# Two pairs of small tables merged, and the weight buffers behind them moved by 64 bytes

## The chip, the core and the metric

The kernel runs on one core of one Trainium2 chip. The metric is the device time of one execution in microseconds. The time before is the median of three runs. One further execution was recorded by the hardware profiler, and all rows below are from that one.

## What is computed

Two transformer-like blocks run one after the other on 256 tokens with 1024 features, all in float32. The first has chunked attention, a gated linear recurrence, a merge of the two branches, and a feed-forward layer; the second has four feed-forward layers, a gating unit with a layer norm over 2048 features, and stick-breaking attention with shared keys and values. Cut to what matters here:

```python
def first_block(x, ...):
    xn = rmsnorm(h, norm_mix_g)
    q, k, v, xr, gr, ga, gb = jnp.split(xn @ w_in, splits, axis=-1)
    ya = chunked_band_attention(q, k, v, rel_table) @ w_attn_out
    hr = rg_lru(causal_depthwise_conv(xr, conv_w, conv_b), ...)
    yb = (hr * jax.nn.gelu(gr)) @ w_rnn_out
    h = h + (g_a * ya + g_b * yb) @ w_o
    g, up = jnp.split(rmsnorm(h, norm_ffn_g) @ w_ffn_in, 2, axis=-1)
    h = h + (jax.nn.silu(g) * up) @ w_ffn_out

def second_block(x, ...):
    # twice: swiglu, then (gating unit | stick-breaking attention), then swiglu
    x = x + 0.5 * swiglu(rms_norm(x, ffn_norm), ffn_w_in, ffn_w_out)
    x = x + chunked_sgu(h, a_w_in, a_ln_g, a_ln_b, a_w_s, a_b_s, a_w_out)
    x = x + stick_breaking_attention(q, k_shared, v_shared) @ b_w_o
```

Nearly all the arithmetic is products of the 256 tokens with large weight matrices.

## The kernel before

Every weight is read once, in 239 pieces of 1 MB (128 partitions x 2048 floats), in an order written out by hand (`PLAN`). `load` (L142 to L150) takes the next of three `raw` buffers and issues its DMA from SyncE. A piece has two chunks of 1024 columns. `prep` (L152 to L171) splits a chunk into two float32r tiles: `h`, a rounded copy that ScalarE makes (L165), and `l`, the difference `raw - h` that VectorE makes (L166). There are eight buffers of `h` and eight of `l`. Splitting runs up to seven chunks ahead of the matmuls.

An activation is split in the same way, into `xh` and `xl`, or into pairs of the four tiles `rr0` to `rr3`. A product is three matmuls that add up in PSUM (`mm3`, L215): high x high, high x low, low x high. All go through `mm` (L213). Rows of the profile name a matmul as out<-moving,stationary. There are two kinds. In `pe_k`, `pe_a` and `pe_r` the weights (`h`, `l`) are stationary, 128 columns of them, and 256 columns of an activation move (`acc<-rr,h`, `wk<-xh,h`). In `pe_nat` and `pe_rn` the activation is stationary and 512 columns of weights move (`wk<-h,xh`, `acc<-h,rr`). In the stage of keys and values (`kv_emit`) both kinds alternate with 256 columns each. Between them stand transposes (L755) and the matmuls of the attentions.

All tiles outside PSUM that live through the kernel come from one pool (`sb`, L133), one behind the other in the order in which the code asks for them: the parameters `par`, the residual `x0` to `x3`, `xh`, `xl`, `rr0` to `rr3`, the slab `sa`, the slabs `sb` to `sh`, two 128x128 tables, and then the small tables, among them `mhalf` (the exponent -0.5 for the power on GpSimd, L283), `tiny` (a bias of the square root at L688), `mv` and `rstd` (mean, variance and its power in the gating unit, L1070 to L1077), and the tables `ntri` and `nones` of the stick-breaking attention. Behind this pool lie the three buffers of `raw`, then the eight of `h`, then the eight of `l`. So the sizes of the small tables decide where the weights lie. An address is a number of bytes inside each partition.

Of the kernel before, what the change touches and what calls it, by code (L numbers as in the profile page):

```python
# [109 lines left out]
class Builder:  # L110
# [210 lines left out]
    def setup(self):  # L321
        nc, dram = self.nc, self.dram
        self.P = self.sb("par", [128, 224])[:, 0:NPAR]
        self.X = [self.sb(f"x{p}", [128, 2, 256]) for p in range(4)]
        self.XS = (self.sb("xh", [128, 8, 256], F32R), self.sb("xl", [128, 8, 256], F32R))
        self.RR = [self.sb(f"rr{i}", [128, 8, 256], F32R) for i in range(4)]
        self.SA = self.sb("sa", [128, 2080])[:, 0:8 * 259]
        self.SL = {c: self.sb("s" + c, [128, 2048]) for c in "bcdfgh"}
        self.ident = self.sb("ident", [128, 128])
        self.ones = self.sb("ones", [128, 128])  # L330
        self.mhalf = self.sb("mhalf", [128, 2])
        self.Rt = self.sb("rt", [128, 256])
        self.R1 = self.sb("r1t", [128, 256])
        self.Rkv = self.sb("rkv", [128, 256])
        self.rckv = self.sb("rckv", [128, 2])
        self.v2 = self.sb("v2", [128, 2])
        self.rc = self.sb("rc", [128, 2])
        self.tiny = self.sb("tiny", [128, 1])
        self.rc05 = self.sb("rc05", [128, 2])
        self.c8 = self.sb("c8", [128, 8])  # L340
        self.nc8 = self.sb("nc8", [128, 8])
        self.half = self.sb("half", [128, 24])
        self.sq = self.view("b", 4)
        nc.scalar.dma_start(self.P, dram["par"])
        x_load = lambda p: nc.sync.dma_start(self.X[p], dram["x"][:, 2 * p:2 * p + 2, :])
        for f in range(2):
            nc.sync.dma_start(self.X[0][:, f, :], dram["x"][:, f, :])
        self.warm_up()
        for g in range(2):
            t = self.rawp.tile([128, 2048], F32, tag="raw", name="raw")  # L350
            for c in range(2):
                if 2 * g + c:
                    x_load(2 * g + c)
                n = 512 if 2 * g + c == 0 else 1024
                for o in range(c * 1024, (c + 1) * 1024, n):
                    nc.sync.dma_start(t[:, o:o + n], dram["w"][g, :, o:o + n])
            self.raw[g] = t
        self.loads = 2
        self.load()
        self.gw = self.SL["h"].rearrange("p (a b) -> p a b", b=128)  # L360
        make_identity(nc, self.ident)
        nc.gpsimd.memset(self.ones, 1.0)
        nc.gpsimd.memset(self.mhalf, -0.5)
        nc.gpsimd.memset(self.tiny, 2.0 ** -115)

    def warm_up(self):
# [658 lines left out]
    def sgu(self, fin, fin_l):  # L1025
        nc, dram, P = self.nc, self.dram, self.par
# [6 lines left out]
        rs = SL["b"][:, 0:1024]  # L1033
        bs = SL["b"][:, 1024:2048]
        st6 = self.sb("bn6", [128, 2, 4, 6])
        mv = self.sb("mv", [128, 2, 2])
        rstd = self.sb("rstd", [128, 2])
        nc.gpsimd.dma_start(ws, dram["ws"])
        nc.gpsimd.affine_select(out=ws, in_=ws, pattern=[[0, 8], [1, 128]], compare_op=ALU.is_ge, fill=0.0,
                                base=0, channel_multiplier=-1)  # L1040
# [54 lines left out]
        a = ("A", "a_in")  # L1095
# [310 lines left out]
```

## Time and profile before

| | |
|---|---|
| time, median of 3 runs | 1444.81 us (1444.66 to 1446.23) |
| the profiled execution, its own time | 1445.04 us |
| its span, first to last instruction | 1443.3 us |
| TensorE busy with matmuls | 1431.0 us, 9112 instructions |
| VectorE busy | 875.1 us |
| ScalarE busy | 732.0 us |
| GpSimd busy | 21.4 us |
| read from HBM | 257.53 MB, 179 GB/s |

Matmuls are pipelined: one is listed from its start to its modelled end, and the next starts long before that. The length of one is therefore not what it costs; the distance from start to start is. Where the chain that ended last shows a run of matmuls without a break, the length of the run over their number is that distance.

### The profile page before, as it was taken

What the parts mean: (1) busy time and instruction counts of PE and PEld (TensorE: products, weight loads), DVE (VectorE), ACT (ScalarE), POOL (GpSimd) and SP (SyncE); (2) the same over time, 40 slices, a digit from 0 to 9 for tenths busy, and PEclk for the clock granted to TensorE, in tenths of its full rate; (3) what the DMA queues carried; (4) which work ended last, traced back from release to release, by engine and by line L of the source; (5) the groups of instructions that cost most, each with busy time, mean ns of one, the idle gap of its engine ahead of it and who ended that gap; (6) DMA issues with size and microseconds to landing.
All of it is one profiled execution on the core that took longest, in us unless ns stands there. A gap on an engine that the chain in (4) does not pass through costs nothing.

```text
span 1443.3 us, 21730 instructions
## 1 busy us (share of the span) xinstructions
PE 1431.0 (99%) x9112; PEld 1277.2 (88%) x9112; DVE 875.1 (61%) x1102; ACT 732.0 (51%) x985; POOL 21.4 (1%) x57
## 2 busy tenths in 40 slices
PE   8999999999999999999999999999999999999998
PEld 8998989888888888898999888898888898888886
DVE  6976688655547555566775554457555477644453
ACT  5777465544445544455444544446444467544442
POOL 0000000000000000000000000000000000000000
PEclk9999999999999999999999999999999999999999
DMA  7555545554553545546444555545554542445440
GB/s 296 197 193 200 186 160 195 188 201 175 184 195 147 204 176 180 209 151 224 171 168 155 222 185 180 191 154 204 186 193 176 183 168 88 161 176 193 186 175 30
DMA packets 37602, 259.98 MB, mean 180 GB/s; under 512 B 4224, under 2 KB 4608, under 8 KB 7040
## 3 DMA queue, kind: packets, MB, share of 16 engines
q1 hardware_dynamic: 36288, 253.77, 48.3%
q0 software_dynamic: 1072, 4.72, 1.0%
q8 instruction: 71, 1.16, 0.3%
q14 instruction: 27, 0.22, 0.0%
q10 hardware_dynamic: 144, 0.10, 0.0%
HBM read 257.53 MB, written 1.05 MB: 179 GB/s over the span
## 4 chain that ended last, share of the span: by engine, by line
PE 97%; DVE 1%; DMA 0%; ACT 0%; issue 0%; POOL 0%; SPq 0%; POOLq 0%; DVEq 0%; ACTq 0%
PE wk L213 60%; PE acc L213 35%; PE wk L755 2%; DMA raw<-w 0%; DVE l L166 0%; PE acc L525 0%; ACT h L165 0%; DVE sd L275 0%; DVE sb L275 0%; PE wk L525 0%; POOL r1c L283 0%; ACT sf L1020 0%; DVE sf L1011 0%; ACT sd L1010 0%; DVE sa L747 0%
## 5 line engine op out<-in xcount | busy, mean ns | idle before, releaser
L166 DVE TENSOR_TENSOR l<-raw,h 128x1024 fp32r<-128x1024 f32 (+1 forms) x479 | 572.7, 1220 | 317.2 <-ACT h L165 316.7
L165 ACT ACTIVATE h<-raw 128x1024 fp32r<-128x1024 f32 (+1 forms) x479 | 495.3, 1053 | 303.5 <-PE wk L213 192.7
L213 PE MATMUL wk<-h,xh 128*128 128x512 f32 x912 | 361.9, 397 | 0.0
L213 PE MATMUL wk<-h,xl 128*128 128x512 f32 x912 | 359.6, 394 | 0.0
L213 PE MATMUL wk<-l,xh 128*128 128x512 f32 x912 | 359.2, 394 | 0.0
L213 PE MATMUL acc<-rr,h 128*128 128x256 f32 x2016 | 358.5, 281 | 0.0
L213 PEld LDWEIGHTS acc<-rr,h 128*128 128x128 f32 x2016 | 307.9, 188 | 3.6 <-issue 1.9
L213 PE MATMUL acc<-rr,l 128*128 128x256 f32 x1008 | 281.2, 279 | 0.0
L213 PEld LDWEIGHTS wk<-h,xl 128*128 128x128 f32 x912 | 171.8, 188 | 39.4
L213 PEld LDWEIGHTS wk<-l,xh 128*128 128x128 f32 x912 | 171.9, 189 | 37.2
L213 PEld LDWEIGHTS wk<-h,xh 128*128 128x128 f32 x912 | 171.9, 188 | 36.8
L213 PEld LDWEIGHTS acc<-rr,l 128*128 128x128 f32 x1008 | 190.0, 189 | 0.0
L213 PE MATMUL wk<-xh,h 128*128 128x256 f32 x512 | 145.5, 284 | 2.0 <-ACT h L165 2.0
L213 PE MATMUL wk<-xh,l 128*128 128x256 f32 x512 | 143.2, 280 | 1.0 <-DVE l L166 1.0
L213 PE MATMUL wk<-xl,h 128*128 128x256 f32 x512 | 143.0, 279 | 0.0
L213 PEld LDWEIGHTS wk<-xh,h 128*128 128x128 f32 x512 | 96.1, 188 | 4.6 <-ACT h L165 2.4
L213 PEld LDWEIGHTS wk<-xh,l 128*128 128x128 f32 x512 | 97.2, 190 | 1.4 <-DVE l L166 1.4
L213 PEld LDWEIGHTS wk<-xl,h 128*128 128x128 f32 x512 | 96.5, 188 | 0.2
L312 ACT ACTIVATE rr<-wk 128x512 fp32r<-128x512 f32 (+1 forms) x63 | 35.9, 569 | 113.9 <-PE wk L755 109.2
L313 DVE TENSOR_TENSOR rr<-wk,rr 128x512 fp32r<-128x512 f32 (+1 forms) x63 | 41.4, 657 | 77.8 <-ACT rr L312 77.8
L743 ACT ACTIVATE sg<-wk,rc 128x512 f32<-128x512 f32 (+1 forms) x48 | 30.8, 652 | 75.6 <-PE wk L213 67.8
L747 DVE SCALAR_TENSOR_TENSOR sa<-wk,rc,sg 128x512 f32<-128x512 f32 (+1 forms) x48 | 32.3, 706 | 53.7 <-PE wk L213 50.0
(256 smaller groups left out, 1167.3 us busy)
## 6 DMA issues: line engine op xcount, KB each, us to landing
raw<-w SPq DMA_DIRECT2D x237, 1024.0 KB, 4.8
sd<-bias POOLq DMA_DIRECT2D x8, 384.0 KB, 3.3
raw<-w SPq DMA_DIRECT2D x3, 512.0 KB, 7.7
sh<-gates SPq DMA_DIRECT2D x1, 1024.0 KB, 9.0
out<-sf SPq DMA_DIRECT2D x4, 256.0 KB, 2.2
x<-x SPq DMA_DIRECT2D x3, 256.0 KB, 6.9
raw<-w SPq DMA_DIRECT2D x2, 256.0 KB, 4.3
sa<-ws POOLq DMA_DIRECT2D x1, 512.0 KB, 5.3
```

What stands on the lines that cost most here:

```text
L165: nc.scalar.activation(h[:, s], raw[:, s], AF.Copy)
L166: nc.vector.tensor_tensor(l[:, s], raw[:, s], h[:, s].bitcast(F32), op=ALU.subtract)
L213: self.nc.tensor.matmul(out, lhsT, rhs, start=start, stop=stop, skip_group_check=True)
L312: self.nc.scalar.activation(zh, src, AF.Copy)
L313: self.nc.vector.tensor_tensor(zl, src, zh.bitcast(F32), op=ALU.subtract)
L743: nc.scalar.activation(SG[i][t][:, 0:w], src, AF.Silu, scale=self.rcol[:, t:t + 1])
L747: nc.vector.scalar_tensor_tensor(Z[i][t][:, 0:w], src, s, SG[i][t][:, 0:w], op0=ALU.mult, op1=ALU.mult)
L755: nc.tensor.transpose(bank[:, f, t * 128:(t + 1) * 128], Z[i][t][:, o:o + 128], self.ident)
```

## The change

The tile `tiny` (one column) becomes the third column of `mhalf`. The tile `rstd` (two columns) becomes the last two of a tile of six columns whose first four are `mv`. The memset of `mhalf` is limited to its first two columns. Every tile that is asked for after these lies lower by what they took, and so do `raw`, `h` and `l`.

```diff
@@ setup @@
-        self.mhalf = self.sb("mhalf", [128, 2])
+        self.mhalf = self.sb("mhalf", [128, 3])
...
-        self.tiny = self.sb("tiny", [128, 1])
+        self.tiny = self.mhalf[:, 2:3]
...
-        nc.gpsimd.memset(self.mhalf, -0.5)
+        nc.gpsimd.memset(self.mhalf[:, 0:2], -0.5)
         nc.gpsimd.memset(self.tiny, 2.0 ** -115)
@@ sgu @@
-        mv = self.sb("mv", [128, 2, 2])
-        rstd = self.sb("rstd", [128, 2])
+        mr = self.sb("mv", [128, 6])
+        mv, rstd = mr[:, 0:4].rearrange("p (a b) -> p a b", b=2), mr[:, 4:6]
```

## Rows read from the trace of the kernel before

**Rows 1.** The page's busy time and chain, and the cores: span, granted clock.
```profile
PE 1431.0 (99%) x9112; PEld 1277.2 (88%) x9112; DVE 875.1 (61%) x1102; ACT 732.0 (51%) x985; POOL 21.4 (1%) x57
...
PE 97%; DVE 1%; DMA 0%; ACT 0%; issue 0%; POOL 0%; SPq 0%; POOLq 0%; DVEq 0%; ACTq 0%
...
core 0: 1443.3 us, clock 0.998
```
**Rows 2.** The chain in order of time: start us, length us, what, number.
```profile
159.75 8.16 PE wk L213 x72
...
334.84 22.40 PE wk L213 x96
...
747.20 36.75 PE acc L213 x312
...
1324.09 21.97 PE wk L213 x96
```
**Rows 3.** Timeline around 300 us: start us, length us, engine, instruction.
```profile
300.50 0.40 PE L213 MATMUL wk<-h,xl 128*128 128x512 f32 x1
300.50 0.19 PEld L213 LDWEIGHTS wk<-h,xh 128*128 128x128 f32 x1
```
**Rows 4.** Groups by line, shapes apart: number | busy us, mean ns | idle.
```profile
L213 PE MATMUL wk<-h,xh 128*128 128x512 f32 x912 | 361.9, 397 | 0.0
...
L213 PE MATMUL acc<-rr,h 128*128 128x256 f32 x2016 | 358.5, 281 | 0.0
...
L213 PE MATMUL acc<-rr,l 128*128 128x256 f32 x1008 | 281.2, 279 | 0.0
...
L213 PE MATMUL wk<-xh,h 128*128 128x256 f32 x512 | 145.5, 284 | 2.0 <-ACT h L165 2.0
...
L213 PE MATMUL acc<-h,rr 128*128 128x512 f32 x176 | 57.7, 397 | 0.0
...
L213 PE MATMUL acc<-l,rr 128*128 128x512 f32 x88 | 34.2, 389 | 0.0
```
**Rows 5.** Timeline of TensorE's matmuls in the stage of keys and values.
```profile
1162.00 0.28 PE L213 MATMUL acc<-rr,l 128*128 128x256 f32 x1
1162.12 0.28 PE L213 MATMUL acc<-h,rr 128*128 128x256 f32 x1
...
1162.83 0.40 PE L213 MATMUL acc<-rr,h 128*128 128x256 f32 x2
...
1163.41 0.28 PE L213 MATMUL acc<-rr,l 128*128 128x256 f32 x1
1163.52 0.28 PE L213 MATMUL acc<-h,rr 128*128 128x256 f32 x1
...
1163.98 0.28 PE L213 MATMUL acc<-l,rr 128*128 128x256 f32 x1
```
**Rows 6.** Single lines of ScalarE and VectorE: ns min/median/max, first and last start.
```profile
L165 ACT ACTIVATE h<-raw x479: 629/1058/1081, 5.9 to 1413.8; 128x1024 fp32r<-128x1024 f32 x159, 128x512 fp32r<-128x512 f32 x1
...
L166 DVE TENSOR_TENSOR l<-raw,h x479: 693/1224/1228, 6.6 to 1415.6; 128x1024 fp32r<-128x1024 f32 x159, 128x512 fp32r<-128x512 f32 x1
...
L682 ACT ACTIVATE sa<-sc x2: 1041/1042/1042, 86.2 to 88.2; 128x1024 f32<-128x1024 f32 x2
...
L684 DVE SCALAR_TENSOR_TENSOR sb<-sa,sb x2: 1217/1218/1220, 90.8 to 93.0; 128x1024 f32<-128x1024 f32 x2
```
**Rows 7.** The tile `rstd`: its writer and its first reader.
```profile
L1077 DVE TENSOR_SCALAR sc<-sc,mv,rstd x4: 539/541/544, 693.1 to 698.9; 128x512 f32<-128x512 f32 x4
...
L283 POOL TENSOR_TENSOR rstd<-v,mhalf x1: 719/719/719, 690.6 to 690.6; 128x2 f32<-128x2 f32 x1
```
**Rows 8.** The chain's first load, and the waits of ScalarE for loads.
```profile
3.14 6.71 DMA raw<-w
...
ACT h L165 <- DMA raw<-w: 9.8, 9, 2.7
```

## The prediction

> **What bounds the kernel now.** I read the page's busy table and its chain first [rows 1]. TensorE is busy for 1431.0 of the 1443.3 us, 97% of the chain that ended last lies on it, and its granted clock was 0.998, so the upper of its two levels, 2.4 GHz. Nothing that happens on another engine or in a queue moves the end unless TensorE waits for it, and TensorE waits almost nowhere. What is left to ask is the pace of the matmuls themselves, so the second view is the chain in order of time, where a piece is a run of matmuls without a break: its length over its count is the pace of one matmul [rows 2].
>
> The pace comes in pairs. With 256 columns it is 8.16 us / 72 = 113.3 ns in one piece and 36.75 / 312 = 117.8 ns in another. With 512 columns it is 21.97 / 96 = 228.9 ns and 22.40 / 96 = 233.3 ns. In the chain a long piece keeps one of the two from end to end and a new one may have the other; in the first four feed-forward stages there are twelve pieces of 96 at 22.40 us, in the last stage three of 96 at 21.97. Two things follow. The quicker and the slower pace differ by the same amount, 4.5 and 4.4 ns, at either length, so it is a charge per matmul and not per column. And 256 more columns cost 228.9 - 113.3 = 115.6 or 233.3 - 117.8 = 115.5 ns, 0.451 ns a column, where one column per cycle would be 1/2.4 = 0.417 ns. Something other than the count of cycles sets the pace, and the operands of these matmuls are just what the change moves.
>
> The third view shows what runs at once: the weight load of the next matmul starts in the same hundredth of a microsecond as the matmul before it [rows 3]. So TensorE reads two streams at a time, the moving operand of one matmul and the stationary operand of the next. In nearly all matmuls one of the two is a split weight (`h`, `l`) and the other an activation (`xh`, `xl`, `rr`).
>
> **The change part by part.** *Does it move them?* Each table takes its bytes per partition rounded up to 32. From `x0` to the first `raw` the sizes add up to 121,408 bytes = 237 x 512 + 64. `mhalf` grows from 8 to 12 bytes and stays in 32, `tiny` goes (-32); `mv` grows from 16 to 24 and stays in 32, `rstd` goes (-32). The sum is then 121,344 = 237 x 512. Buffers of `raw` are 8192 bytes apart, those of `h` and `l` 4096, so all 19 move with it. `x`, `xh`, `xl`, `rr`, `sa` and the `s` slabs lie ahead of the small tables and stay. `ntri` and `nones` move by 32 bytes; they serve 64 matmuls only.
>
> *Instructions.* None is added or removed. The two POOL memsets of `mhalf` and `tiny` stay two. The only new ties are that a reader of one half of a merged table may be held for the writer of the other half. For `mhalf`/`tiny` both writers are memsets at the start. For `mv`/`rstd` the power on POOL starts at 690.6 us for 719 ns and needs the variance made from `mv` anyway; its first reader on VectorE starts at 693.1 us [rows 7]. That leaves 693.1 - 691.3 = 1.8 us, so an added tie costs 0; without that cover it would be below 1 us, once.
>
> *The split on ScalarE and VectorE.* 479 copies `h<-raw` have a median of 1058 ns, 479 differences `l<-raw,h` one of 1224 ns, at 64 past. The nearest rows with other places in the 512 bytes are a 128x1024 copy-like activation from 128 past to 0 past, 1041 to 1042 ns, and a 128x1024 VectorE operation at 128 and 0 past, 1217 to 1220 ns [rows 6]. At most the change gives back 16 and 6 ns a piece, or takes as much: 479 x 0.016 = 7.7 us on ScalarE, which has 48% of the span free. On the path stands one such pair, ahead of the first matmul: 0.02 us. I take 0.
>
> *The loads.* 1 MB loads write rows of 8 KB at the new place. ScalarE waited for `raw` 9.8 us in total, 9 times, and on the chain a load stands once, 6.71 us at the start [rows 8]. A load dearer or cheaper by 1% would be 0.07 us there. I take 0.
>
> *The matmuls.* These carry the sum. With 256 columns there are 2016 + 1008 + 3 x 512 [rows 4], and in seven smaller groups of the same kind 192 + 96 + 3 x 64 + 32 + 16: 5088. With 512 there are 3 x 912 + 176 + 88 and three groups of 64: 3192. If each pace held half of them, they would take 5088 x 115.55 + 3192 x 231.1 = 587.9 + 737.7 = 1325.6 us of the span (an estimate: the pieces show both paces in like amounts). All at the quicker pace they would take 576.5 + 730.6 = 1307.1 us, 18.5 less; all at the slower 599.4 + 744.7 = 1344.1 us, 18.5 more. With one column per cycle, 106.7 and 213.3 ns, they would take 542.9 + 680.9 = 1223.8 us, 101.8 less. So the bounds of this term are -102 and +18.5 us, and all hangs on whether a place in the 512 bytes matters to the pace.
>
> For that the trace has three rows that bear on it. First, absolute place: in the 256-column runs the moving operand is at 0 and the stationary one at 64, in the 512-column runs the other way round, and both show the same two paces, 4.4 ns apart. In the `kv` stage the same 256 columns stand both ways side by side [rows 5]: with `h` and `l` moving, six matmuls in 1162.83 - 1162.12 = 0.71 us, 118 ns; on the next pass four in 1163.98 - 1163.52 = 0.46 us, 115 ns; and the six with `rr` moving between them take 0.69 us, 115 ns. So which of the two lies at 64 is all one. Second, relative place: only at a handover are both streams at 0, when `rr,l` runs while the weights of `h,rr` load. It took 0.12 us in the slower stretch and 0.11 us in the quicker [rows 5], what its neighbours took. One matmul with both at the same place is thus neither freed of the charge nor charged more. Third, against that: the pace turns over just there, from 118 ns before 1162.83 to 115 ns on the mean of the six after it, so a step in the relative place may well choose which pace is kept. I take 0 for the term, nearest to the handovers, with -18.5 and +18.5 us as its ends, since those are paces that the trace shows to last.
>
> The Trainium skill, "SBUF — State Buffer", section "Who interferes with whom", says that TensorE waits on no other engine and that its two read ports are independent; by it the place is worth 0 us. Rows 2 agree only in part: 0.451 ns a column is not what two undisturbed ports would give. The same skill, "TensorE: Matmul & The Clock Gate", section "Back-to-back issue gap", gives N/2.4 + 2.5 ns warm, 109.2 and 215.8 ns; if the place were the whole excess, the sum by that figure would be 5088 x 6.4 + 3192 x 15.3 = 81 us less (an estimate from that page).
>
> **The rivals.** *Quicker.* With both streams at a multiple of 512, TensorE falls into the quicker pace after each break. For it speaks that the pace is chosen at a break or a change of relative place and kept; against it that a handover in the slower stretch cost 0.12 us. All of it is worth 18.5 us, 1426.3; half of it 1435.6. Inside it lies the case that the excess goes altogether (to 1343), for which no row speaks; I give it 0.03, within the 0.36 below.
>
> *Slower.* Stream and load start together [rows 3], and after the change they start at the same place of their 512 bytes, in every matmul. If two reads of one place hold each other up, each start pays the 4.4 ns and the slower pace holds all through: 1463.3, half of it 1454.0. It decides as soon as 2.9 / 0.00445 = 650 of the 8280 matmuls change to the slower pace. The 0.12 us handover speaks for it, the 0.11 us one against.
>
> *The change doesn't do what it says*, because tables are packed more coarsely than 32 bytes: then nothing moves, 1444.8. The sum of sizes comes out at 64 with 32, so I give it 0.02, within the forecast.
>
> **How the numbers follow.** The profiled run took 1445.04 us, 1443.3 of span and 1.7 around it; the median of the three runs is 1444.81, so the sum of 0 on the profiled run is 1444.8 for the median. The forecast, no place matters or the paces stay mixed as they are: 0.39, 1442 to 1447.7. Quicker: 0.36, nearly all of it between 1426 and 1441.9. Slower: 0.25, between 1447.7 and 1463. A measurement can tell about 0.2%, 2.9 us, from no change, which is where the three are parted. The range runs from 1425 to 1460: it leaves out the loss of the whole excess, and the last of the slower end.
>
> **What would show it.** Right: pieces of the chain still at 113.3 or 117.8 and 228.9 or 233.3 ns, in like amounts, and medians of the two split operations within 16 ns. Quicker: 22.40 us pieces of 96 turn to 21.97 and the 36.75 us piece of 312 to about 35.4. Slower: the reverse, and 8.16 us for 72 turns to 8.48. Paces that are none of the four would show that the relative place enters the pace itself, which I have not allowed for except in the ends. A wait before the power on POOL at 690.6 us, or a longer first load, would show the small terms wrong.

## The result, and the profile after

The changed kernel takes 1453.63 us (median of 4 runs, 1453.34 to 1455.03) beside 1444.77 for the kernel before on the same chip. The ratio is 1.0061, with a 95% interval of 1.0044 to 1.0078. The change costs 8.9 us.

| | before | after |
|---|---|---|
| time, median | 1444.77 us | 1453.63 us |
| span of the profiled execution | 1443.3 us | 1452.1 us |
| 256 columns, pace in long pieces | 113.3 or 117.8 ns | 120.0 ns |
| 512 columns, pace in long pieces | 228.9 or 233.3 ns | 226.7 to 227.0 ns |

The page after, beside [rows 1]: the head of the page, its busy table, the shares of the chain that ended last, and the row of the core.

```profile
span 1452.1 us, 21730 instructions
...
PE 1440.0 (99%) x9112; PEld 1296.2 (89%) x9112; DVE 875.8 (60%) x1102; ACT 731.8 (50%) x985; POOL 22.4 (2%) x57
...
PE 98%; DVE 1%; ACT 0%; DMA 0%; issue 0%; POOL 0%; SPq 0%; POOLq 0%; DVEq 0%; ACTq 0%
...
core 0: 1452.1 us, clock 0.998
```

No engine but TensorE moved by more than 1.0 us, the counts of [rows 1] are the same, and the granted clock is the same 0.998, the upper level. TensorE is busy 9.0 us longer, the span is 8.8 us longer. So the pace of the matmuls has to be read again. These are the pieces of the chain after that answer to [rows 2] (start us, length us, what, number):

```profile
162.92 8.64 PE wk L213 x72
...
341.67 21.79 PE wk L213 x96
...
755.07 37.44 PE acc L213 x312
...
1333.51 21.76 PE wk L213 x96
```

With 256 columns the pace is 8.64 / 72 = 120.0 and 37.44 / 312 = 120.0 ns: it was 113.3 in the first of the two and 117.8 in the second. With 512 columns it is 21.79 / 96 = 227.0 and 21.76 / 96 = 226.7 ns: it was 233.3 and 228.9. Neither number is one of the four paces of before. The weights lie now at the same place of 256 bytes as the activations, and both kinds have left their two paces for a single new one, the shorter matmul for a dearer one and the longer for a cheaper one.

The two make the result. With the means that the prediction used, 5088 x (120.0 - 115.55) = +22.6 us and 3192 x (226.7 - 231.1) = -14.0 us, together +8.6 us (an estimate). Added up from start to start over all matmuls of the two traces, those of 256 columns took 19.0 us more, those of 512 columns 11.0 us less and the rest 0.8 us more: these are the 8.8 us by which the span grew.

The timeline of TensorE's matmuls in the stage of keys and values, after, beside [rows 5]:

```profile
1171.40 0.40 PE L213 MATMUL acc<-rr,h 128*128 128x256 f32 x2
...
1172.12 0.28 PE L213 MATMUL acc<-h,rr 128*128 128x256 f32 x1
...
1172.84 0.40 PE L213 MATMUL acc<-rr,h 128*128 128x256 f32 x2
```

Six matmuls with `rr` moving take 1172.12 - 1171.40 = 0.72 us, and the six with `h` and `l` moving take 1172.84 - 1172.12 = 0.72 us: 120 ns both ways round, and at the handovers too. So the new pace belongs to the length of the matmul and to where the two streams stand to each other, and not to which of them holds the weights.

The other steps of the prediction show in these rows after: the split on ScalarE and VectorE beside [rows 6], then the power on GpSimd and its first reader beside [rows 7].

```profile
L165 ACT ACTIVATE h<-raw x479: 629/1057/1080, 6.8 to 1422.6; 128x1024 fp32r<-128x1024 f32 x159, 128x512 fp32r<-128x512 f32 x1
...
L166 DVE TENSOR_TENSOR l<-raw,h x479: 693/1224/1229, 7.5 to 1424.4; 128x1024 fp32r<-128x1024 f32 x159, 128x512 fp32r<-128x512 f32 x1
...
L1077 DVE TENSOR_SCALAR sc<-sc,mv x4: 540/542/544, 699.7 to 705.5; 128x512 f32<-128x512 f32 x4
...
L283 POOL TENSOR_TENSOR mv<-v,mhalf x1: 719/719/719, 696.9 to 696.9; 128x2 f32<-128x2 f32 x1
```

The medians are 1057 and 1224 ns, where they were 1058 and 1224. The power ends at 697.6 us and its first reader starts at 699.7, so nothing waits for the merged table.

### The profile page after: what moved, and what is told of

Its sections match the earlier page's. It is cut to its first block, busy times and chain, and to the rows that moved or that the text cites. A ratio compares the mean times of both kernels' runs of the same rounds, so it can differ in the third digit from the quotient of the medians.

```text
span 1452.1 us, 21730 instructions
## 1 busy us (share of the span) xinstructions
PE 1440.0 (99%) x9112; PEld 1296.2 (89%) x9112; DVE 875.8 (60%) x1102; ACT 731.8 (50%) x985; POOL 22.4 (2%) x57
## 4 chain that ended last, share of the span: by engine, by line
PE 98%; DVE 1%; ACT 0%; DMA 0%; issue 0%; POOL 0%; SPq 0%; POOLq 0%; DVEq 0%; ACTq 0%
PE wk L213 60%; PE acc L213 36%; PE wk L755 2%; DMA raw<-w 0%; DVE l L166 0%; PE acc L525 0%; DVE sd L275 0%; DVE sb L275 0%; PE wk L525 0%; ACT h L165 0%; POOL r1c L283 0%; ACT sf L1020 0%; DVE sf L1011 0%; ACT sd L1010 0%; DVE sa L747 0%
## 5 line engine op out<-in xcount | busy, mean ns | idle before, releaser
L213 PE MATMUL acc<-rr,h 128*128 128x256 f32 x2016 | 370.1, 285 | 0.0
L213 PE MATMUL wk<-h,xh 128*128 128x512 f32 x912 | 357.5, 392 | 0.0
L213 PE MATMUL wk<-l,xh 128*128 128x512 f32 x912 | 355.2, 389 | 0.0
L213 PE MATMUL wk<-h,xl 128*128 128x512 f32 x912 | 355.1, 389 | 0.0
L213 PEld LDWEIGHTS acc<-rr,h 128*128 128x128 f32 x2016 | 315.2, 192 | 3.5 <-issue 1.9
L213 PE MATMUL acc<-rr,l 128*128 128x256 f32 x1008 | 285.2, 283 | 0.0
L213 PEld LDWEIGHTS acc<-rr,l 128*128 128x128 f32 x1008 | 193.2, 192 | 0.0
L213 PE MATMUL acc<-h,rr 128*128 128x512 f32 (+1 forms) x208 | 64.4, 378 | 0.0
```

The source lines that it names most:

```text
L213: self.nc.tensor.matmul(out, lhsT, rhs, start=start, stop=stop, skip_group_check=True)
```

## The experiments

Three theories stood at the start. A: the relative place of the two streams sets the pace, with a period of 128 bytes. B: the same, but only a step of 512 bytes counts as the same place. C: the place matters for another engine (a split, a load), and TensorE only shows it. Here "distance" is the place of the split weights minus the place of the activation, in bytes. It is 64 in the kernel before and 0 after.

### The matmuls alone, at many distances

> Leaves out the whole computation: only matmuls of the kernel's two kinds, nothing beside them on ScalarE, VectorE or the queues. 42 blocks; in each the weights h and l are read from 16 bytes further on than in the block before (0 to 512 bytes past a multiple of 512), the activations stay at a multiple of 512; then once more in steps of 64. A block is 48 matmuls of 256 columns (weights stationary) and 24 of 512 (weights moving). Theory A, the pace hangs on the distance of the two streams within 128 bytes: 120.0 and 226.7 ns at 0, 128, 256, 384, 512, and the paces of the kernel before (113.3 or 117.8; 228.9 or 233.3) at 64, 192, 320, 448. Rival B, multiples of 512 are the special case: 120.0 and 226.7 at 0 and 512 only. Rival C, the change of pace came from what runs beside the matmuls (the splits, the loads): flat over all offsets.

The kernel has 42 blocks like these, with nothing beside them (cut: the choice of `out` and `ts` and the start and stop flags are left out); only the first column `c` of the weights moves, by 16 bytes from block to block (0 to 512), then once more by 64 bytes:

```python
def rows(c):                       # 48 matmuls of 256 columns
    for k in range(2):
        for i in range(8):
            s = slice(i * 128 + c, i * 128 + c + 128)
            mm(out, h[:, s], xh[:, k, :]); mm(out, h[:, s], xl[:, k, :]); mm(out, l[:, s], xh[:, k, :])
def nat(c):                        # 24 matmuls of 512 columns
    for k in range(4):
        s = slice((k % 2) * 512 + c, (k % 2) * 512 + c + 512)
        for t in range(2):
            mm(out, xh[:, k, ts], h[:, s]); mm(out, xh[:, k, ts], l[:, s]); mm(out, xl[:, k, ts], h[:, s])
```

Pieces of the chain at the distances 64, 256, 512, and at 64 and 128 on the second pass:

```profile
59.18 5.45 PE acc L40 x48
64.63 5.49 PE wk L40 x24
...
194.10 5.76 PE acc L40 x48
199.86 5.47 PE wk L40 x24
...
373.98 5.76 PE acc L40 x48
379.74 5.47 PE wk L40 x24
...
396.43 5.65 PE acc L40 x48
402.08 5.60 PE wk L40 x24
407.69 5.70 PE acc L40 x48
413.39 5.57 PE wk L40 x24
```

At 256 and at 512 the pair is 5.76 / 48 = 120.0 and 5.47 / 24 = 227.9 ns (the first five matmuls of such a block of 24 are still slower, the others are at 226.7), the paces of the changed kernel. At 64 (and in the same way at 320) it is 113.5 and 228.8 ns, the quicker paces of the kernel before. At 64 on the second pass it is 117.7 and 233.3 ns, the slower paces of the kernel before. So all six paces of the two kernels come from the two streams alone, with no other engine at work: theory C falls. The pattern repeats after 256 bytes: 256 does what 512 does, and at 128 the 512-column block takes 5.57 us, not the 5.47 of the distance 0, which theory A excludes. Theory B falls with the row at 256. And the distance 64 has two pairs of paces.

| distance in bytes | 48 of 256 columns | 24 of 512 columns |
|---|---|---|
| 0 | 5.75 us | 5.47 us |
| 32 | 5.67 | 5.59 |
| 64 | 5.45 or 5.65 | 5.49 or 5.60 |
| 112 | 5.76 | 5.45 |
| 128 | 5.70 | 5.57 |
| 192 | 5.66 | 5.60 |
| 208 | 5.60 | 5.63 |
| 240 | 5.63 | 5.67 |

The table shows eight of the sixteen distances tried below 256. No simple rule is seen in it: 112 gives the pair of 0, while 240 has the dearest 512-column pace of all, 5.67 / 24 = 236.3 ns.

### Only the split weights moved back

`raw` stays at its new place and the tables stay merged; 64 unused bytes stand between `raw` and `h`. Two more kernels do the same with 128 and 32 bytes.

```diff
+            tc.tile_pool(name="gap", bufs=1) as gp, \
...
+        nc.gpsimd.memset(gp.tile([128, 16], F32, tag="gap", name="gap"), 0.0)
```

> The changed kernel with 64 unused bytes between raw and h: raw at 0 past a multiple of 512, h and l at 64 as before the change; the merged tables stay. Theory A: the matmuls go back to 113.3 or 117.8 and 228.9 or 233.3 ns, 1443 to 1447 us. Rival: the place of raw, or the merged tables, made the loss: 1453.6 us stays.

Measured: 1444.72 us, 1.0003 times the kernel before (0.9993 to 1.0012). The chain of this kernel, same two places:

```profile
334.69 22.40 PE wk L213 x96
...
747.06 36.75 PE acc L213 x312
```

These are the lengths of [rows 2] to the hundredth. The whole loss hangs on where `h` and `l` lie; the merged tables, their ties and the place of `raw` cost nothing that can be measured.

> The changed kernel with 128 unused bytes between raw and h: h and l at 128. Theory A (only the distance within 128 bytes counts): 120.0 and 226.7 ns, 1452 to 1455 us. Rival B (multiples of 512 are special): the paces of the kernel before, 1443 to 1447 us.

Measured: 1465.86 us, ratio 1.0146 (1.0131 to 1.0161), a span of 1464.6.

```profile
163.14 8.54 PE wk L213 x72
...
342.05 22.32 PE wk L213 x96
...
759.54 37.44 PE acc L213 x312
```

The 512-column pace is 22.32 / 96 = 232.5 ns, the 256-column one 8.54 / 72 = 118.6 in the first piece and 37.44 / 312 = 120.0 in the last. The matmuls alone show 232 and 119 at 128; the 120.0 of the long piece they don't show, so at 128 too there is more than one pace. The time is neither 1452 to 1455 (A) nor 1443 to 1447 us (B).

> The changed kernel with 32 unused bytes between raw and h: h and l at 32. Theory A, with paces that move in steps with the distance, expects paces that are none of the six seen so far, between those of 0 and of 64 or outside them: 1430 to 1475 us, not 1453.6 and not 1444.8 within 2 us. Rival, only whole steps of 64 bytes count: 1453.6 as at 0.

Measured: 1463.89 us, ratio 1.0134 (1.0118 to 1.0149), a span of 1462.3.

```profile
340.78 22.39 PE wk L213 x96
...
757.74 36.92 PE acc L213 x312
```

The paces are 233.2 and 118.3 ns. With the means of before, 5088 x (118.3 - 115.55) + 3192 x (233.2 - 231.1) = 14.0 + 6.7 = 20.7 us (an estimate); the span grew by 19.0. A distance that is quick for neither kind costs twice as much as the change did.

### Relative or absolute, and how a pace is chosen

> Leaves out the whole computation: only matmuls. First part, 17 blocks of 48 matmuls of 256 columns and 24 of 512, with h and l read from c and the activations from d bytes past a multiple of 512: c = d = 0; c = d = 0, 64, 128, 192; c = 0 and d = 0, 64, 128, 192; d = 64 and c = 0, 64, 128, 192; c = d once more. Second part, 16 blocks of 48 matmuls of 256 columns with c = 64, d = 0, each behind one lone matmul of 16, 32, ... 256 columns. Theory A, only the distance moving minus stationary counts, within 256 bytes: all c = d give 120.0 and 226.7 ns; c = 0, d = 64 is what the first sweep had at 192 (117.8 and 233.3); c = 0, d = 192 what it had at 64 (113.3 or 117.8, 228.9 or 233.3). Rival, the place of h and l itself counts: c = d = 64 as the first sweep at 64, and c = 0 always 120.0 and 226.7. Second part: theory A says that the entry chooses between the two paces, so both 5.44 and 5.65 us per block appear; rival, chance or the kind of matmul before: one of them only, or without order.

Here the activations move too (`d` bytes) beside the weights (`c` bytes). Pieces of the chain for (c, d) = (192, 192), (0, 64), (0, 192), (128, 64), in this order:

```profile
59.22 5.75 PE acc L42 x48
64.97 5.47 PE wk L42 x24
...
81.65 5.65 PE acc L42 x48
87.30 5.60 PE wk L42 x24
...
104.17 5.45 PE acc L42 x48
109.62 5.49 PE wk L42 x24
...
137.58 5.66 PE acc L42 x48
143.24 5.60 PE wk L42 x24
```

Both streams moved together change nothing: 5.75 and 5.47 us at 192 as at 0, 64 and 128. Weights at 0 with activations at 192, a distance of 64 modulo 256, give the quick pair that weights at 64 give. So the distance modulo 256 bytes is what counts, and the place of one stream alone doesn't. The last pair has the distance 64 again, and the slower of its two pairs.

The second half of this kernel asks what picks one of the two. Sixteen blocks of 48 at the distance 64 follow, each behind one lone matmul of 16, 32, ... 256 columns. The ones at 32 and 48 columns, and the start of the next:

```profile
210.74 0.01 PE wk L42
210.75 5.56 PE acc L42 x48
216.31 0.02 PE wk L42
216.33 5.74 PE acc L42 x48
222.07 0.03 PE wk L42
```

From the start of a lone matmul to the start of the next it is 5.57 us (32 columns) or 5.76 us (48). Of the 16 blocks 8 run at the quicker pace and 8 at the slower, and none between: behind 32, 64, 80, 96, 144, 176, 192 and 224 columns quick, behind the others slow. What one matmul did ahead of the block holds to the block's end: read from start to start, the slow ones run at 118 ns from their second matmul on, the quick ones at 113 or 114 ns from their seventh at the latest.

### One kind of matmul given the distance that suits it

Before, with `xh` and `xl` of the feed-forward stages 64 bytes higher (one tile, 64 columns wider so that what lies behind it keeps its place modulo 256, used at two offsets of 0 and 16 columns; the lines that choose between them by stage are left out here). The 512-column matmuls then have the distance 0, the 256-column ones keep 64:

```diff
-        self.XS = (self.sb("xh", [128, 8, 256], F32R), self.sb("xl", [128, 8, 256], F32R))
+        xs = self.sb("xh", [128, 4096 + 64], F32R)
+        self.XS0, self.XS1 = (tuple(xs[:, o + 2048 * i:o + 2048 * i + 2048].rearrange("p (a b) -> p a b", b=256)
+                                    for i in range(2)) for o in (0, 16))
...
```

> The kernel before, with the activations of the five feed-forward layers 64 bytes further on (the split xh and xl of those stages alone), so that their 512-column matmuls have both streams at the same place, while the 256-column matmuls keep their distance of 64. Theory A: 2640 matmuls of 512 columns at 226.7 ns in place of 228.9 and 233.3, 7.6 us from the twelve pieces at 233.3 and 3.7 us from the rest; the 256-column ones of these stages keep 113.3 or 117.8, in some other mixture (up to 5 us either way): 1429 to 1440 us. Rival, one pace for both kinds that goes with the layout as a whole: 1444.8 or 1453.6.

Measured: 1439.63 us, ratio 0.9965 (0.9952 to 0.9978), a span of 1439.4.

```profile
337.06 21.77 PE wk L213 x96
358.83 5.66 PE acc L213 x48
```

The 512-column pace is 21.77 / 96 = 226.8 ns, as meant, and yet the span fell by only 3.9 us. Part of the gain was given back in the next piece: the 48 matmuls of 256 columns behind such a run take 5.66 us. In the kernel before 18 of the 20 such pieces took 5.46 or 5.47, in this one all 20 take 5.66: 18 x 0.19 = 3.4 us. The distance of these 48 had not changed; what they enter from had. Added up from start to start, the 512-column matmuls took 10.3 us less, the 256-column ones with `rr` moving 4.8 us more (these 3.4 among them) and those with `xh` and `xl` 1.6 us more. The profiled execution took 1441.06 us, above the median; by the medians the gain is 5.2 us.

The other way round, the changed kernel with `rr0` to `rr3` at 192 of 256, so that 3312 of the 256-column matmuls have the distance 64 back:

```diff
+        nc.gpsimd.memset(self.sb("gap", [128, 48]), 0.0)
         self.RR = [self.sb(f"rr{i}", [128, 8, 256], F32R) for i in range(4)]
+        nc.gpsimd.memset(self.sb("gap2", [128, 16]), 0.0)
```

> The changed kernel, with the tiles rr0 to rr3 192 bytes past a multiple of 256 in place of 0 (h and l, xh and xl stay at 0 of 256), so that 3312 of the 256-column matmuls have the distance of 64 that they had before the change, and the 512-column ones keep 0, but for 264 in the last stage. Theory A: 3312 matmuls go from 120.0 to 113.3 or 117.8 ns, 7 to 22 us less, and 264 from 226.7 to 228.9 or 233.3, 0.6 to 1.7 us more: 1432 to 1448 us. Rival, the place of h and l alone: 1453.6.

Measured: 1441.99 us, ratio 0.9982 (0.9973 to 0.9992), a span of 1440.1.

```profile
161.16 8.62 PE wk L213 x72
...
338.48 21.76 PE wk L213 x96
...
749.06 35.37 PE acc L213 x312
```

Where `rr` moves, 35.37 / 312 = 113.4 ns; where `xh` moves, still 8.62 / 72 = 119.7 ns, since it wasn't moved.

Both together, with `xh` and `xl` at 192 where 256 columns move and at 0 in the feed-forward stages:

```diff
+        xs = self.sb("xh", [128, 4096 + 48], F32R)
+        self.XS0, self.XS1 = (tuple(xs[:, o + 2048 * i:o + 2048 * i + 2048].rearrange("p (a b) -> p a b", b=256)
+                                    for i in range(2)) for o in (48, 0))
...
+        nc.gpsimd.memset(self.sb("gap2", [128, 16]), 0.0)
```

> The changed kernel with rr0 to rr3 at 192 past a multiple of 256 bytes, and with xh and xl twice in one tile 48 columns wider: at 192 past where 256 columns move over a split weight, at 0 where they are stationary under 512 moving columns of weights. So every matmul of 256 columns has the distance of the kernel before (64) and every one of 512 columns that of the changed kernel (0). If the distance modulo 256 bytes alone sets which paces there are, the first kind runs at 113.3 or 117.8 ns (5088 of them) and the second at 226.7: 1440 at 192-byte rr less 1776 x 2.2 to 6.7 ns = 3.9 to 11.9 us, so 1430 to 1438 us. Rival: the absolute place counts too, so that something else than these three paces shows and the time is above 1438 us.

Measured: 1435.29 us, ratio 0.9935 (0.9921 to 0.9948), a span of 1433.0.

```profile
159.15 8.16 PE wk L213 x72
...
333.87 21.76 PE wk L213 x96
355.63 5.66 PE acc L213 x48
```

The paces are 113.3 ns where `xh` moves and 226.7 ns in the feed-forward stage, and again it is 5.66 us for the 48 behind the 512-column run, all 20 times. The matmuls alone did the same: the three of their blocks at the distance 64 that stand right behind a 512-column run at the distance 0 were slower ones too. Not all 512-column matmuls were given the distance 0, as the expectation has it: the 264 of the last stage that have `rr` stationary keep 64, and a piece of 24 of them takes 5.50 us, 229.2 ns. No pace appears that the matmuls alone hadn't shown.

### Choosing the pace on entry

> As the run with both shifts, but in each of the four feed-forward stages with 256 columns moving over the output weights, the first matmul of each group of 48 is cut in two: w and 256 - w columns, w = 32, 64, 96, 128, 160, 192, 224 by the group's number. Theory (the pace at distance 64 is chosen by how the streams stand to each other at entry, and kept): some widths turn the run from 117.8 to 113.3 ns, the same ones in each of the four stages, so pieces of 49 of about 5.57 us beside others of about 5.77. Rival: behind 512-column matmuls at 226.7 ns the slower pace follows whatever the width: all at about 5.77. The 28 added matmuls cost up to 28 x 0.12 = 3.4 us, and half the groups at the quicker pace give back 2.9.

```diff
+            if o == 0 and cut:
+                self.mm(out[:, 0:cut], h[:, s], zh[:, 0:cut], start, False)
+                self.mm(out[:, cut:256], h[:, s], zh[:, cut:256], False, False)
...
```

The five groups of 48 of a feed-forward stage got the widths 32, 64, 128, 192 and 32. The chain of the first stage shows them in this order:

```profile
293.33 5.57 PE acc L215 x49
...
321.63 5.76 PE acc L215 x49
...
355.71 5.56 PE acc L215 x49
...
389.59 5.56 PE acc L215 x49
...
423.47 5.57 PE acc L215 x49
```

All four stages show the same five lengths within 0.01 us. With 32, 128 and 192 columns first the group turns to the quicker pace, with 64 it stays at the slower, every time in this execution, so the choice is hardly chance. Nor is it the width by itself: as lone matmuls ahead of a block, 64 columns gave the quicker pace and 128 the slower. The kernel's one run took 1436.03 us, no less than without cuts: 40 matmuls were added (not 28, as written ahead), 20 of them in groups that don't stand behind a 512-column run, and a cut that doesn't turn its group costs 5.76 - 5.66 = 0.10 us.

> As the run with both shifts, and the first matmul of the five groups of 48 in each of the four feed-forward stages (20 in all) cut into 32 and 224 columns, and none elsewhere. If the entry chooses the pace, all 20 pieces of 49 take about 5.57 us instead of 5.66 for 48: 20 x 0.09 = 1.8 us less, a span of 1431.2 beside the 1433.0 of the run with both shifts. Rival: the width that turns a group depends on the group, so that some of the 20, above all the second of each stage (tried with 64 only), stay at 5.76 and the span is about 1432 to 1435.

Measured: 1431.63 us, ratio 0.9904 (0.9888 to 0.9921), and a span of 1431.2 us, the number expected.

```profile
span 1431.2 us, 21771 instructions
...
321.72 5.57 PE acc L213 x49
```

All 20 pieces of 49 take 5.57 us, the second of each stage too, now that it has 32 columns. In part the agreement of the spans is luck: the profiled execution is the longest of four here (1432.87 us) and was the shortest of five with both shifts (1434.74 us). By the medians the gain is 3.7 us, twice what was expected, and where the rest of it comes from isn't shown. This is the fastest kernel of the study, 13.3 us below the kernel before and 22.0 below the changed one, with nothing changed but places in SBUF (for which one memset of unused bytes was added) and 20 matmuls cut in two.

## Why the prediction was wrong

*What bounds the kernel* was right: TensorE stands for 98% of the chain after, and all but 0.8 us of the 8.8 is in the pace of the matmuls over split weights.

*Whether anything moves* was right: 64 bytes put back ahead of `h` and `l` bring back 1444.72 us and the lengths of [rows 2].

*Instructions, ties, split and loads at 0* were right. 21730 instructions before and after; the power on GpSimd has 2.1 us to spare before its reader; the split's medians moved by 1 and 0 ns, where the bounds were 16 and 6; ScalarE waited 11.4 us for loads instead of 9.8 [rows 8], off the path.

*The matmul term taken as 0* is the step that failed. Its parts came out like this:

- "So which of the two lies at 64 is all one", the argument on absolute place, holds so far as both streams moved together leave the pace where it was. That the two may be swapped isn't shown: at the distance 192, the activations 64 bytes above the weights, all six blocks of the matmuls alone show the slower pair.
- "One matmul with both at the same place is thus neither freed of the charge nor charged more" fails, and all hung on it. It took the 0.12 and 0.11 us of a single handover [rows 5] for what a run of such matmuls would take. The timeline shows hundredths of a microsecond; 113.3, 117.8 and 120.0 ns can't be told apart in them, and the difference to be judged was 4.5 ns, 22.6 us over 5088 matmuls. Nor is one matmul a run: read to the nanosecond, the two handovers took 120 and 113 ns, while after the change every matmul of that stretch takes 120; what the entry does is seen in the whole piece behind it. A row for a 256-column run at the distance 0 wasn't in the trace, and for a 512-column one there was no handover at all.
- "A step in the relative place may well choose which pace is kept" was the better reading of the same rows, and it is what the runs show: with the same distance, 48 matmuls take 5.46 or 5.66 us, by what went before.
- The ends of the term, -18.5 and +18.5 us, came from giving both kinds the same fate, because the same 4.4 ns part the paces of either. That was the second fault: at the distance 0 the 256-column matmul is 2.2 ns slower than its slower pace, and the 512-column one 2.2 ns quicker than its quicker pace. The net (+19.0 and -11.0 us from start to start) lies inside the ends, but by cancellation and not by the reasons given.

*The rivals.* The forecast was no change, 1444.8 us; 1453.63 lies inside the stated range only because the range took in the rivals. "Slower" had the sign and half its price near the result (1454.0), but not the mechanism: it said 117.8 and 233.3 ns for all, and no long piece after has either. "Quicker" gave its 512-column pieces 21.97 us; they took 21.79, and the 256-column ones lost more than these won. The prediction's own test, paces that are none of the four, is what came; no rival stood for it. The mechanism that was missing is a pace that depends on the distance and on the length of the matmul together.

The Trainium skill, "SBUF — State Buffer", section "Who interferes with whom", says that the two read ports of TensorE are independent; that the place is worth 0 us by it, as the prediction read it, doesn't agree with these runs: the distance moved the span by +8.8, +21.3 and +19.0 us. The excess didn't vanish at any distance tried either: the lowest paces in any run are 113.3 and 226.7 ns, above the 109.2 and 215.8 that "TensorE: Matmul & The Clock Gate", section "Back-to-back issue gap", gives as isolated spacing.

What stays open: why two streams at a given distance hold each other up by just so much, and by what rule a short matmul on entry picks one of two paces. The runs show that it does, repeatably, for the widths tried; a width was found by trying, and none was predicted.

## What to carry to other kernels

Before a float32r kernel that is bound by TensorE gets or loses a small tile, work out where the split operands lie modulo 256 bytes and read each kind's pace from long pieces of the chain (length over count); 32 to 128 bytes in front of the buffers were worth 0.6 to 1.5% here. Choose the distance for each kind of matmul by itself: here 0 for 512 columns moving and 64 for 256. Don't take one interval of the timeline for a pace, and when a gain comes out small, look at the first long piece behind the one that was improved.

## What the runs showed of the hardware that wasn't expected

- The pace of float32r matmuls depends on the distance of the split weights and the activation modulo 256 bytes: 113.3 to 120.0 ns with 256 columns, 226.7 to 236.3 ns with 512, with no other engine at work. The best distances for 512 columns (0 and 112) are among the dearest for 256.
- At the distance 64 two paces are stable, 113.3 and 117.8 ns, and what goes before, the length of a single matmul among it, picks one. Either held over a piece of 312 matmuls, the slower in the kernel before and the quicker with `rr` at 192.
- A short matmul with its own 128 columns of weights is nearly as dear as a long one: a lone one of 32 columns and the block behind it took 5.57 us, of which 48 x 113.3 ns = 5.44 are the block, so 0.13 us (the block's first matmuls, not yet at its pace, are in it); one of 48 columns 5.76 - 48 x 117.8 ns = 0.11 us, where a full one at that pace takes 0.118.
- For ScalarE and VectorE operands at 0 or at 64 made no difference that could be measured: 1057 beside 1058 ns and 1224 beside 1224 ns for the two halves of the split, where all three tiles move together, and 1058 and 1224 ns with `raw` at 0 and `h` and `l` at 64.
